# S5 chunk states: rows of 32 neighbouring groups for each chunk, in place of rows of chunks for each group

## The chip, the core and the metric

The kernel runs on one core of a Trainium2 chip. The metric is the device time in microseconds (us) of one execution of the whole program, in fp32; the median of three runs of the kernel before is 1691.3 us (1687.9 to 1693.93). The engines named below are PE (TensorE; PEld is its loading of the stationary operand, which runs beside PE), DVE (VectorE), ACT (ScalarE), POOL (GpSimd) and SP (SyncE, which here only issues DMAs).

## What is computed

One inference step of a trunk of four layers (S5, RetNet, Hyena, S5) on 128 context tokens and 256 latent tokens, 384 columns in all, with a model width of 1024. The change touches the two S5 layers (layer 0 and layer 3) alone. There the 1024 channels form 64 groups of 16, and each group drives a complex diagonal state of 64 numbers in two directions:

```python
bu_re = jnp.einsum('blgh,gph->blgp', u, bb_re)      # and bu_im
_, _, h_re, h_im = lax.associative_scan(combine, (a_re, a_im, bu_re, bu_im), axis=1)
y = (jnp.einsum('blgp,ghp->blgh', h_re, c_re) - jnp.einsum('blgp,ghp->blgh', h_im, c_im))
```

The second direction does the same on the reversed sequence, and the result is y of both plus d times u.

## The kernel before

**Chunks.** An S5 layer cuts the 384 tokens into 48 chunks of 8 (`NCH = 48`; the first `CC = 16` are context). Within a chunk the sum is a Toeplitz matmul; between chunks a state of 128 numbers (64 complex ones) for each group and direction is carried. These chunk states are the tile X. There are two halves of it (`Xs[0]` and `Xs[1]`, 32 groups each, `XH = 32`), and each is 128 partitions by 64 rows (2 directions times 32 groups) by `XP = 49` columns (chunk boundaries). So one group's states over all chunks lie side by side, and the states of neighbouring groups at one chunk are 49 numbers (196 bytes) apart.

**Who touches X, in order.**
- `use_p(b)` (one for every 8 groups) makes each chunk's own contribution: matmuls of U with PB (line 746), copies to Ss (line 748, ACT), transposes (line 755, PE), and a copy from PSUM into X (line 758, ACT: 384 numbers for each partition, 32 copies in both layers).
- `recur(q)` (line 769, once for each half q) carries the states from chunk to chunk on DVE. One round is line 792 (a shuffle that swaps real and imaginary parts, X to sw), 793 (X times A1 to m1), 794 (add m1 to the next X), 795 (sw times A2) and 796 (add sw to the next X), each on 64 numbers for each partition: 32 groups in two directions. There are 47 rounds in a call (31 for the latent chunks, 16 for the context), 188 in both layers. Context and latent rounds do not depend on each other and alternate until the context is done. A context's last round writes XF, a small tile of 64 neighbouring numbers, instead of X, and line 797 sends it out on the ACT queue.
- Lines 880 to 882 make y: for every group a matmul with U (880), one with X of the first direction (881) and one with X of the second (882). X is the stationary operand there: 48 columns, the states of one group at 48 chunks.

**What sets the order.** The program is written as plans (`PLAN0`, `PLAN1`): P is `use_p`, R is `recur`, U the input projection. R0 (half 0) stands after P3, R1 (half 1) after P7. The half's last copy (line 758) releases `recur`. After the plan come the gate matmuls (line 138, with line 161's cast on ACT, line 133's remainder on POOL, line 530 on ACT and line 531 on DVE for each of 8 blocks), which don't need X, and then lines 880 to 882. A scheduler with a timing model of its own places the instructions of each engine's queue; every queue then runs in its order. In layer 0 the DVE also makes CP (lines 628 and 629, `gen_c`), whose sums are added by DMAs issued on POOL (line 631) and whose inputs xc are loaded on the SP queue (line 686), between weight loads (line 152) and loads of Tt (line 850).

Of the kernel before, what the change touches and what calls it, by code (L numbers as in the profile page):

```python
# [10 lines left out]
F32 = mybir.dt.float32  # L11
# [15 lines left out]
NCH = T // Q  # L27
XP = NCH + 1
CC = NCTX // Q
# [7 lines left out]
NH = 2  # L37
# [67 lines left out]
def hybrid_trunk(ctx: ExitStack, tc: tile.TileContext, I, O, dbg=None, layers=(0, 1, 2, 3)):  # L105
    nc = tc.nc
    V, S, G, TE = nc.vector, nc.scalar, nc.gpsimd, nc.tensor
# [13 lines left out]
    def psm():  # L121
        return pm.tile([128, 512], F32, tag="m", name="psm")
# [9 lines left out]
    def gstt(out, a, b, op):  # L132
        G.tensor_tensor(out, a, b, op=op)  # L133
# [218 lines left out]
    def tick(n=1):  # L352
        for _ in range(n):
            if bg:
                bg.popleft()()
# [328 lines left out]
    def gen_c(j, hb, tb, rot, CP, xb, eng=V, add=G):  # L684
        xc = rot.tile([128, 2, 2, 4, 16], F32, tag="xc", name="xc")
        nc.sync.dma_start(xc, I["s5bc"][j, hb // 4, :, hb % 4, 1])
        expand_c(CP, rot, tb, xc, hb, xb, eng, add)
# [10 lines left out]
    def s5(i, j, nxt, begun=lambda: None):  # L698
        def mk(st, name, bufs=1, **kw):
            return st.enter_context(tc.tile_pool(name=f"{name}_{i}", bufs=bufs, reuse_waits="tile", **kw))  # L700
        ep = ExitStack()
        eU = ExitStack()
        pool = mk(eU, "s5", side="right") if j == 0 else mk(ep, "s5")
        U = pool.tile([128, 8, 8 * NCH + 16], F32, name="U")
        XH = 64 // NH
        Xs = [pool.tile([128, 2 * XH, XP], F32, name=f"X{q}") for q in range(NH)]
        XFs = [pool.tile([128, 2, XH], F32, name=f"XF{q}") for q in range(NH)]
        hpool = mk(ep, "s5h")
        h0 = load(pool, "h0", I["s5h0"][j], eng=nc.scalar)
# [29 lines left out]
        def use_p(b):  # L739
            Ss = ru.tile([128, 2, 512], F32, tag="Ss", name="Ss", bufs=1)  # L740
            for r in range(2):
                PB = PBs.pop(2 * b + r)
                ps = psm()
                for g in range(4):
                    o = 64 * (g % 2)
                    mark[0] = TE.matmul(ps[o:o + 64, (g // 2) * 256:(g // 2) * 256 + 256], U[:, b, (r * 4 + g) * NCH:(r * 4 + g) * NCH + 64],  # L746
                              PB[:, g].rearrange("p a b -> p (a b)"), start=True, stop=True)
                S.copy(Ss[:, r], ps)
            for hf in range(2):
                ps = psm()  # L750
                o = 64 * hf
                for g in range(4):
                    for d in range(2):
                        c = (g % 2) * 256 + d * 128
                        TE.transpose(ps[:, (d * 4 + g) * 64:(d * 4 + g) * 64 + 48],  # L755
                                     Ss[o:o + 48, g // 2, c:c + 128], ident[o:o + 48, o:o + 48])
                xb = Xs[b * 8 // XH][:, b * 8 % XH + hf, 1:2]
                S.copy(bass.AP(tensor=xb.tensor, offset=xb.offset,
                               ap=[xb.ap[0], [XH * XP - 1, 2], [2 * XP, 4], [1, NCH]]),
                       ps.rearrange("p (d g c) -> p d g c", d=2, g=4)[:, :, :, :48])  # L760

        def u_epi(m, ps):
# [7 lines left out]
        def recur(q):  # L770
            gs = slice(q * XH, (q + 1) * XH)
            A1, A2 = Av[:, 0, :, gs], Av[:, 1, :, gs]
            X, XF = Xs[q], XFs[q]
            Xb = X[:, 0, 0:1]
            V.tensor_copy(XF[:, 0], X[:, 0:XH, CC])
            V.tensor_copy(XF[:, 1], X[:, XH:2 * XH, 0])

            def view(c_f, c_b):
                return bass.AP(tensor=Xb.tensor, offset=Xb.offset + c_f,
                               ap=[Xb.ap[0], [XH * XP + c_b - c_f, 2], [XP, XH]])  # L780
            V.memset(view(0, CC), 0.0)
            V.tensor_copy(view(CC, NCH), h0.rearrange("p (d g) -> p d g", d=2)[:, :, gs])
            for k in range(NCH - CC - 1):
                for c0, n in ((CC, NCH - CC), (0, CC)):
                    if k >= n:
                        continue
                    c1 = c0 + n - 1
                    cur = view(c0 + k, c1 - k + 1)
                    dst = XF if k == n - 1 else view(c0 + k + 1, c1 - k)
                    sw = tmp.tile([128, 2, XH], F32, tag=f"sw{c0}{q}", name="sw")  # L790
                    m1 = tmp.tile([128, 2, XH], F32, tag=f"m1{c0}{q}", name="m1")
                    V.stream_shuffle(sw, cur, [(x + 16) % 32 for x in range(32)])  # L792
                    V.tensor_mul(m1, cur, A1)  # L793
                    V.tensor_add(dst, dst, m1)  # L794
                    V.tensor_mul(sw, sw, A2)  # L795
                    V.tensor_add(dst, dst, sw)  # L796
            nc.scalar.dma_start(O["ns5"][j].rearrange("p (d g) -> p d g", d=2)[:, :, gs], XF)
# [47 lines left out]
        def toeplitz(m):  # L845
            kdm = I["kd"][j * 8 + m]
            Tt = rot.tile([128, 8, 128], F32, tag="Tt", name="Tt")
            for t in range(8):
                src = bass.AP(tensor=kdm.tensor, offset=kdm.offset + (7 - t) * 16, ap=[[1920, 16], [240, 8], [1, 128]])
                nc.sync.dma_start(Tt[16 * t:16 * t + 16], src)  # L850
            Tm = rot.tile([128, 8, 128], F32, tag="Tm", name="Tm", bufs=TMB)
            for r in range(2):
                ps = psm()
                for g in range(4):
                    TE.transpose(ps[:, g * 128:(g + 1) * 128], Tt[:, r * 4 + g, :], ident)  # L855
                S.copy(Tm[:, r * 4:r * 4 + 4, :], ps.rearrange("p (g c) -> p g c", c=128))
            Tms.append(Tm)
        for m in range(TMB):
            toeplitz(m)
        for m in range(8):  # L860
            CP = []
            for r in range(2):
                c = rot.tile([128, 2, 4, 8, 16], F32, tag="CP", name="CP", bufs=CPB if j == 0 else CP1)
                if j == 0 and 2 * m + r not in SPL:
                    gen_c(j, 2 * m + r, tb, rot, c, 2, V, None)
                else:
                    (CQ if j else nc.sync).dma_start(c.rearrange("p d g e c -> p (d g e c)"), I["cpd"][2 * m + r])
                CP.append(c)
            Tm = Tms[m]
            hf = m % 2  # L870
            if hf == 0:
                pys = [psm(), psm()]
                Ys = rot.tile([128, 8, 8, 16], F32, tag="Ys", name="Ys", bufs=1)
            for r in range(2):
                for g in range(4):
                    gl = r * 4 + g
                    gg = m * 8 + gl
                    o = pys[r][64 * hf:64 * hf + 64, g * 128:(g + 1) * 128]
                    o48 = pys[r][64 * hf:64 * hf + 48, g * 128:(g + 1) * 128]
                    TE.matmul(o, U[:, m, gl * NCH:gl * NCH + 64], Tm[:, gl, :], start=True, stop=False)  # L880
                    TE.matmul(o48, Xs[gg // XH][:, gg % XH, 0:48], CP[r][:, 0, g].rearrange("p a b -> p (a b)"), start=False, stop=False)  # L881
                    TE.matmul(o48, Xs[gg // XH][:, XH + gg % XH, 1:49], CP[r][:, 1, g].rearrange("p a b -> p (a b)"), start=False, stop=True)  # L882
            if m + TMB < 8:
                toeplitz(m + TMB)
            tick(CT)
            if hf == 0:
                continue
            for r in range(2):
                S.copy(Ys[:, :, r * 4:r * 4 + 4, :], pys[r].rearrange("p (g t i) -> p t g i", g=4, t=8))
            for hf in range(2):  # L890
                fb = m - 1 + hf
                o = 64 * hf
                pg = psm()
                for t in range(8):
                    TE.transpose(pg[:, t * 64:t * 64 + 48], Ys[o:o + 48, t].rearrange("p a b -> p (a b)"),  # L895
                                 ident[o:o + 48, o:o + 48])
                y = pg.rearrange("p (t c) -> p c t", t=8)[:, :48, :]
                x2 = t384("gx2").rearrange("p (c t) -> p c t", t=8)
                gf = t384("gf")
                gv = gf.rearrange("p (c t) -> p c t", t=8)  # L900
                S.activation(x2, y, AF.Square, scale=math.sqrt(0.044715))
                V.scalar_tensor_tensor(x2, x2, 1.0, y, op0=OP.add, op1=OP.mult)
                S.activation(x2, x2, AF.Tanh, scale=math.sqrt(2.0 / math.pi))
                V.scalar_tensor_tensor(gv, x2, 1.0, y, op0=OP.add, op1=OP.mult)
                put(g_parts, fb, gf)
                gstt(sgate[:, fb, :], gf, sgate[:, fb, :], OP.mult)
# [670 lines left out]
```

## Time and profile before

| what | us |
|---|---|
| median of three runs | 1691.3 |
| the profiled execution | 1695.14 |
| its span, first to last instruction | 1693.3 |
| PE busy in it | 1488.7 (88%) |
| DVE busy in it | 1288.4 (76%) |
| ACT busy, POOL busy | 688.8 (41%), 660.6 (39%) |

The span is divided by layer: layer 0 runs to about 420 us, layer 3 from about 1400 us to the end. A share of the whole span says little here, since the two stages with the recurrence (about 167 to 326 us and 1466 to 1572 us) have other limits than the dense matmuls that fill the rest. They are read by windows, by the instructions' durations line by line, and by what PE waited for.

### The profile page before, as it was taken

The page shows a single profiled execution, that of the slowest core. Times are in us where ns is not written, and L with a number is a line of the kernel's source. Part 1 is how long each engine was busy: PE and PEld are TensorE (multiplying, and loading weights), DVE is VectorE, ACT ScalarE, POOL GpSimd, SP SyncE. Part 2 cuts the span into 40 slices and gives each one's busy share as a digit, 9 for nine tenths or more (in the row PEclk, how much of TensorE's full clock was granted, in tenths as well). Part 3 has the DMA queues.
Part 4 walks back from the last instruction along what each step waited for, and adds up shares of the span by engine and source line. Part 5 has one row for each costly group of instructions (what it writes and reads, how often), then busy time and mean ns, then how long its engine had stood idle before and what let it go on. Part 6 is the DMA issues. An engine that isn't in the chain of part 4 may idle for free. (4 is left out here: it accounts for less than half of the span.)

```text
span 1693.3 us, 27807 instructions
## 1 busy us (share of the span) xinstructions
PE 1488.7 (88%) x10370; PEld 1320.6 (78%) x10370; DVE 1288.4 (76%) x3123; ACT 688.8 (41%) x1275; POOL 660.6 (39%) x484
## 2 busy tenths in 40 slices
PE   5778776799689998999979999999999998976996
PEld 3555564677579888889969989989899797675996
DVE  8957998569787777755878988888798855399355
ACT  2534321333333333335455545454555444421343
POOL 2111231213375756651325655655576131230221
PEclk7888887899899999999989999999999999987998
DMA  8578469844555555544333222222322463755431
GB/s 346 172 227 242 132 167 256 206 144 174 187 173 200 189 198 189 179 152 135 130 114 111 87 75 83 97 94 78 100 88 80 145 240 110 239 145 179 125 125 63
DMA packets 107807, 261.41 MB, mean 154 GB/s; under 512 B 28535, under 2 KB 68568, under 8 KB 88088
## 3 DMA queue, kind: packets, MB, share of 16 engines
q1 hardware_dynamic: 80768, 200.12, 36.1%
q0 software_dynamic: 11984, 34.87, 7.5%
q10 hardware_dynamic: 14920, 24.65, 4.0%
q8 instruction: 82, 1.34, 0.3%
q14 instruction: 53, 0.43, 0.1%
HBM read 220.37 MB, written 30.83 MB: 148 GB/s over the span
## 5 line engine op out<-in xcount | busy, mean ns | idle before, releaser
L133 POOL TENSOR_TENSOR wl<-wr,wh 128x1024 fp32r<-128x1024 f32 (+2 forms) x99 | 248.3, 2513 | 322.2 <-ACT wh L161 294.4
L161 ACT CAST wh<-wr 128x1024 fp32r<-128x1024 f32 (+4 forms) x211 | 215.7, 1029 | 292.7 <-PE psd L138 215.2
L138 PE MATMUL psd<-hh,wh 128*128 128x384 f32 x880 | 305.9, 349 | 17.6 <-ACT wh L161 7.5
L138 PE MATMUL psd<-hh,wl 128*128 128x384 f32 x880 | 304.5, 347 | 11.2 <-POOL wl L133 8.8
L138 PE MATMUL psd<-hl,wh 128*128 128x384 f32 x880 | 304.6, 346 | 6.5 <-DVE hl L469 6.4
L148 DVE TENSOR_TENSOR wl<-wr,wh 128x1024 fp32r<-128x1024 f32 (+3 forms) x112 | 146.4, 1309 | 73.3 <-ACT wh L161 72.8
L138 PEld LDWEIGHTS psd<-hh,wh 128*128 128x128 f32 x880 | 169.1, 193 | 29.6 <-issue 12.9
L138 PEld LDWEIGHTS psd<-hh,wl 128*128 128x128 f32 x880 | 169.1, 192 | 20.1 <-POOL wl L133 10.5
L138 PEld LDWEIGHTS psd<-hl,wh 128*128 128x128 f32 x880 | 169.1, 192 | 15.8 <-DVE hl L469 9.2
L138 PE MATMUL psd<-wl,hh 128*128 128x256 f32 x384 | 110.3, 289 | 5.2 <-DVE wl L148 3.8
L138 PE MATMUL psd<-wh,hh 128*128 128x256 f32 x384 | 110.9, 293 | 4.1 <-DVE g L531 2.8
L138 PE MATMUL psd<-wh,hl 128*128 128x256 f32 x384 | 109.0, 286 | 0.0
L378 PE MATMUL psn<-wr,sgc 128*32 128x256 f32 x640 | 58.3, 450 | 45.4 <-DMA wr<-in_mod_w_dram 37.9
L138 PE MATMUL psd<-zb,wh 128*128 128x384 f32 x240 | 80.9, 338 | 0.0
L138 PEld LDWEIGHTS psd<-wl,hh 128*128 128x128 f32 x384 | 74.1, 193 | 6.9 <-DVE wl L148 4.7
L138 PEld LDWEIGHTS psd<-wh,hh 128*128 128x128 f32 x384 | 73.6, 193 | 6.2 <-DVE g L531 3.5
L138 PEld LDWEIGHTS psd<-wh,hl 128*128 128x128 f32 x384 | 74.1, 193 | 0.1
L629 DVE TENSOR_TENSOR xt<-BI,xc 128x512 f32<-128x512 f32 x52 | 45.2, 870 | 37.0 <-POOL CP L633 16.6
L378 PEld LDWEIGHTS psn<-wr,sgc 128*32 128x32 f32 x640 | 20.0, 121 | 67.3 <-DMA wr<-in_mod_w_dram 41.2
L633 POOL TENSOR_TENSOR BP<-BP,xt 128x512 f32<-128x512 f32 x32 | 46.0, 1437 | 63.7 <-DVE xt L629 37.7
L629 DVE TENSOR_TENSOR xt<-FI,bc 128x512 f32<-128x512 f32 x64 | 48.8, 768 | 26.7 <-DMA CP<-xt 9.0
L631 POOL DMA_DIRECT2D CP<-xt x32 | 27.6, 905 | 101.0 <-DVE X L796 28.7
(388 smaller groups left out, 4069.6 us busy)
## 6 DMA issues: line engine op xcount, KB each, us to landing
wr<-in_mod_w_dram SPq DMA_DIRECT2D x40, 1024.0 KB
wr<-in_hy_w_in_dram SPq DMA_DIRECT2D x32, 1024.0 KB
wr<-in_ret_w_in_dram SPq DMA_DIRECT2D x24, 1024.0 KB
wr<-in_s_w_in_dram SPq DMA_DIRECT2D x16, 1024.0 KB
wm<-in_mod_w_dram SPq DMA_DIRECT2D x8, 1024.0 KB
CP<-xt POOLq DMA_DIRECT2D x32, 256.0 KB, 7.2
Tt<-scratch_kd_dram SPq DMA_DIRECT2D x128, 64.0 KB
wr<-in_s_w_glu_dram SPq DMA_DIRECT2D x8, 1024.0 KB
```

The source lines that it names most:

```text
L133: G.tensor_tensor(out, a, b, op=op)
L138: TE.matmul(out, lhs[a], rhs[b], start=start and i == 0, stop=stop and i == len(combos) - 1)
L148: V.tensor_sub(out, a, b)
L161: S.copy(hi, ap)
L378: TE.matmul(ps[q * 32:(q + 1) * 32, :256], sg[:, kb, 6 - 2 * u:38 - 2 * u], raw[:, kb, :], start=u == 0 and k2 == 0, stop=u == 3 and k2 == 1)
L629: eng.tensor_tensor(t, c2, x[:, 1].unsqueeze(2).to_broadcast([128, 4, 8, 16]), op=OP.mult)
L631: nc.gpsimd.dma_start(out, t, accum_op=OP.add)
L633: add.tensor_tensor(out, out, t, op=OP.add)
```

## The change

X gets the index order direction, chunk, group: 128 partitions by 2 by 49 by 32. The 32 groups of one chunk and direction are now 32 neighbouring numbers, and one group's consecutive chunks are 32 numbers (128 bytes) apart. The size is the same. All that reads or writes X follows: the ACT copy of line 758 writes runs of 48 with a step of 32 where it wrote neighbouring numbers; all DVE operands of `recur` on X are two runs of 32 neighbours where they were 64 single numbers 49 apart; the stationary operand of lines 881 and 882 is 48 numbers with a step of 32 where it was 48 neighbours. No instruction is added or removed.

```diff
-        Xs = [pool.tile([128, 2 * XH, XP], F32, name=f"X{q}") for q in range(NH)]
+        Xs = [pool.tile([128, 2, XP, XH], F32, name=f"X{q}") for q in range(NH)]
...
-                xb = Xs[b * 8 // XH][:, b * 8 % XH + hf, 1:2]
+                xb = Xs[b * 8 // XH][:, 0, 1:2, b * 8 % XH + hf]
                 S.copy(bass.AP(tensor=xb.tensor, offset=xb.offset,
-                               ap=[xb.ap[0], [XH * XP - 1, 2], [2 * XP, 4], [1, NCH]]),
+                               ap=[xb.ap[0], [(XP - 1) * XH, 2], [2, 4], [XH, NCH]]),
                        ps.rearrange("p (d g c) -> p d g c", d=2, g=4)[:, :, :, :48])
...
-            Xb = X[:, 0, 0:1]
-            V.tensor_copy(XF[:, 0], X[:, 0:XH, CC])
-            V.tensor_copy(XF[:, 1], X[:, XH:2 * XH, 0])
+            Xb = X[:, 0, 0, 0:1]
+            V.tensor_copy(XF[:, 0], X[:, 0, CC])
+            V.tensor_copy(XF[:, 1], X[:, 1, 0])
 
             def view(c_f, c_b):
-                return bass.AP(tensor=Xb.tensor, offset=Xb.offset + c_f,
-                               ap=[Xb.ap[0], [XH * XP + c_b - c_f, 2], [XP, XH]])
+                return bass.AP(tensor=Xb.tensor, offset=Xb.offset + c_f * XH,
+                               ap=[Xb.ap[0], [(XP + c_b - c_f) * XH, 2], [1, XH]])
...
-                    TE.matmul(o48, Xs[gg // XH][:, gg % XH, 0:48], CP[r][:, 0, g].rearrange("p a b -> p (a b)"), start=False, stop=False)
-                    TE.matmul(o48, Xs[gg // XH][:, XH + gg % XH, 1:49], CP[r][:, 1, g].rearrange("p a b -> p (a b)"), start=False, stop=True)
+                    TE.matmul(o48, Xs[gg // XH][:, 0, 0:48, gg % XH], CP[r][:, 0, g].rearrange("p a b -> p (a b)"), start=False, stop=False)
+                    TE.matmul(o48, Xs[gg // XH][:, 1, 1:49, gg % XH], CP[r][:, 1, g].rearrange("p a b -> p (a b)"), start=False, stop=True)
```

The scheduler orders some instructions anew. Two places matter for the prediction. The first is DVE in layer 3, where R1 (half 1, X1_14481) begins among the rounds of R0 (half 0, X0_14480). The kernel before, from a round of R0 to the first rounds of both:

```order
L794 TENSOR_TENSOR X0_14480<-X0_14480,m1_15057 128x2x32
L796 TENSOR_TENSOR X0_14480<-X0_14480,sw_15063 128x2x32
L775 COPY XF1_14483<-X1_14481 128x32
L776 COPY XF1_14483<-X1_14481 128x32
L781 MEMSET X1_14481 128x2x32
L796 TENSOR_TENSOR X0_14480<-X0_14480,sw_15056 128x2x32
L792 STREAM_SHUFFLE sw_15077<-X0_14480 128x64
```

The same place in the changed kernel:

```order
L795 TENSOR_TENSOR sw_15070<-sw_15070,A1_4514 128x64
L794 TENSOR_TENSOR X0_14480<-X0_14480,m1_15071 128x2x32
L775 COPY XF1_14483<-X1_14481 128x32
L776 COPY XF1_14483<-X1_14481 128x32
L781 MEMSET X1_14481 128x2x32
L796 TENSOR_TENSOR X0_14480<-X0_14480,sw_15077 128x2x32
L796 TENSOR_TENSOR X0_14480<-X0_14480,sw_15070 128x2x32
```

R1's first copy stands behind 22 rounds of R0 before and behind 24 now. From there to R0's last round 60 rounds of either half follow before (25 of R0, 35 of R1) and 57 now (23 and 34); 12 rounds of R1 come last before, 13 now. In layer 0, 79 rounds stand from R0's first to its last, before and now.

The second place is the ACT queue of layer 3 at the gate blocks, where the issue of line 797 (which waits for half 0's context states, XF0) moves behind one more block (lines 161 and 530):

```order
 L530 ACTIVATE silu_15849<-psd_15820 128x384
+L161 CAST wh_15921<-wr_15918 128x1024
+L530 ACTIVATE silu_15883<-psd_15854 128x384
+L856 COPY Tm_16111<-psm_16112 128x512
 L797 DMA out_ns5_dram<-XF0_14482 256x1x32
-L530 ACTIVATE silu_15883<-psd_15854 128x384
-L161 CAST wh_15921<-wr_15918 128x1024
+L856 COPY Tm_16111<-psm_16118 128x512
 L161 CAST wh_15953<-wr_15918 128x1024
```

The third block's cast and activation stood behind line 797's wait and now stand ahead of it.

## Rows read from the trace of the kernel before

**Rows 1.** Windows: stretch, its length, busy PE, PEld, DVE, ACT, POOL, clock, DMA share, GB/s.

```profile
240.00:275.00 35.00, 16.77 (x104) 12.98 (x104) 33.84 (x154) 1.36 (x3) 10.62 (x9) 0.67 0.79 203
270.00:280.00 10.00, 3.56 (x24) 2.17 (x25) 9.89 (x60) 0.00 (x0) 1.70 (x2) 0.50 1.02 290
1520.00:1548.00 28.00, 20.03 (x146) 15.09 (x144) 28.00 (x164) 3.59 (x6) 4.23 (x2) 0.89 0.70 204
1548.00:1572.00 24.00, 18.05 (x150) 17.41 (x151) 21.20 (x124) 7.12 (x14) 3.06 (x5) 0.77 0.56 156
```

**Rows 2.** Instructions by line, DVE: count, minimum/median/maximum ns, first and last start.

```profile
L793 DVE TENSOR_TENSOR m<-X,A x188: 239/255/2344, 169.0 to 1570.3; 128x64 f32<-128x64 f32 x188
L794 DVE TENSOR_TENSOR X<-X,m x184: 250/266/5432, 174.4 to 1571.1; 128x64 f32<-128x64 f32 x184
L794 DVE TENSOR_TENSOR XF<-XF,m x4: 218/228/233, 211.4 to 1546.6; 128x64 f32<-128x64 f32 x4
L781 DVE MEMSET X<- x4: 112/112/112, 167.4 to 1487.6; 128x64 f32 x4
L338 DVE MEMSET ones<- x1: 165/165/165, 0.8 to 0.8; 128x128 f32 x1
```

**Rows 3.** Timeline of DVE, one round of R1 alone: start us, us, what.

```profile
1559.82 0.26 DVE L792 STREAM_SHUFFLE sw<-X 128x64 f32<-128x64 f32 x1
1560.00 0.26 DVE L793 TENSOR_TENSOR m<-X,A 128x64 f32<-128x64 f32 x1
1560.17 0.22 DVE L795 TENSOR_TENSOR sw<-sw,A 128x64 f32<-128x64 f32 x1
1560.30 0.27 DVE L794 TENSOR_TENSOR X<-X,m 128x64 f32<-128x64 f32 x1
...
1560.92 0.26 DVE L792 STREAM_SHUFFLE sw<-X 128x64 f32<-128x64 f32 x1
```

**Rows 4.** Layer 3: shuffles until R1 begins; timeline, with idle time before and its releaser.

```profile
L792 DVE STREAM_SHUFFLE sw<-X x22: 248/254/272, 1466.8 to 1486.1; 128x64 f32<-128x64 f32 x22
...
1485.27 1.00 ACT L758 COPY X<-psm 128x384 f32<-128x384 f32 x2 [3.40 <-PE psm L755]
1487.31 0.17 DVE L775 COPY XF<-X 128x32 f32<-128x32 f32 x1
1509.68 0.49 ACT L530 ACTIVATE silu<-psd 128x384 f32<-128x384 f32 x1 [17.52 <-DVE X L796]
1554.97 0.66 PE L881 MATMUL psm<-CP,X 128*48 128x128 f32 x2 [4.78 <-DVE X L796]
1571.70 0.57 DVE L796 TENSOR_TENSOR X<-X,sw 128x64 f32<-128x64 f32 x1
1574.94 0.38 PE L881 MATMUL psm<-CP,X 128*48 128x128 f32 x2
```

**Rows 5.** Layer 0: timeline of PE at the first use of X; waits of SP's queue.

```profile
275.34 1.94 PE L378 MATMUL psn<-wr,sgc 128*32 128x256 f32 x16 [8.03 <-DMA wr<-in_mod_w_dram]
278.37 0.66 PE L881 MATMUL psm<-CP,X 128*48 128x128 f32 x2 [1.10 <-DVE X L796]
...
SPq L686 <- DVE X L794: 10.9, 1, 10.9
```

**Rows 6.** Stationary loads and ACT copies by line (as rows 2); two steps of PE's timeline.

```profile
L881 PEld LDWEIGHTS psm<-CP,X x256: 119/123/203, 278.4 to 1609.9; 128*48 128x48 f32 x128
L1253 PEld LDWEIGHTS psm<-ident,ac x96: 138/196/217, 889.5 to 1345.1; 128*128 128x128 f32 x96
L764 ACT COPY us<-psd x14: 469/479/491, 75.9 to 1467.4; 128x384 f32<-128x384 f32 x14
L764 ACT COPY us<-xb x2: 925/931/937, 1433.8 to 1434.7; 128x384 f32<-128x384 f32 x2
...
296.57 0.38 PE L882 MATMUL psm<-CP,X 128*48 128x128 f32 x2
296.79 0.38 PE L880 MATMUL psm<-Tm,U 128*64 128x128 f32 x2
```

## The prediction, made before the changed kernel ran

> **What bounds the kernel now.** I read the windows of the two stages with the recurrence first, then the durations of the recurrence's instructions, then what PE waited for when it first needed X. In [rows 1] DVE is busy for 33.84 of 35 us in layer 0 and for all 28 us of a stretch of layer 3, while PE, which bounds most of the kernel, is busy for 16.77 and 20.03 us. So here, and only here, DVE sets the pace. The reader should then see where that ends. In layer 3 PE's first matmul with X starts at 1554.97 after 4.78 us of waiting for line 796, the last add of the recurrence [rows 4]: all that follows hangs on R0's end. R1's end, at 1571.70 + 0.57 = 1572.3, is needed by the matmul at 1574.94, so it has 2.7 us to spare. In layer 0 the same first matmul waited only 1.10 us for DVE, right behind 8.03 us for a weight load [rows 5], with the DMA engines fully busy there (share 1.02, [rows 1]); DVE is one of two late things.
>
> **What the change takes off DVE.** Every round reads or writes X four times (lines 792, 793, 794, 796). The trace has the same instructions on neighbouring numbers. Line 794 takes 266 ns on X and 228 ns where it works on XF [rows 2]; line 793, which only reads X, takes 255, and line 795, on two neighbouring operands, 0.22 us [rows 3]. Instructions on DVE overlap, so what counts is the step from one start to the next. In [rows 3] the steps are 0.18 after the shuffle, 0.17 after line 793, and 0.13 after line 795, the one without X. So X costs 0.045 us a step, four times a round: 0.18 us of a round that takes 1.10 us alone (1559.82 to 1560.92). No row has a shuffle on neighbours in SBUF; its gain lies between 0 and 0.045, and I take 0.045, since it reads X exactly as line 793 does. With 0 a round would gain 0.135. For 188 rounds that is 25 to 34 us of DVE; the rest is where these rounds stand.
>
> **Layer 3.** R0's 22 rounds up to R1's start run from 1466.8 to 1487.31, some 0.85 us each apart from one 2 us stall [rows 4]. With 24 rounds of 0.67 us and that stall DVE reaches R1 at about 1485, but R1 needs the last copies of line 758, which PE's own work releases and which end at 1486.27 [rows 4]. So R1 starts 1.0 us earlier and the rest of that gain is lost in a wait. From there to R0's end before were 1554.97 - 1487.31 = 67.7 us with 60 rounds; now there are 57. Three rounds fewer are 2.5 us (0.84 each), and 57 x 0.18 = 10.3. Together 1.0 + 2.5 + 10.3 = 13.8 us, with 0.135 a round 11.2. For PE to take it, its gate blocks must be ready 9 us earlier than now (13.8 less the 4.78 us that it waited). They wait for DVE's line 531, which comes earlier with the rounds, and for ACT, which stood 17.52 us behind line 797 [rows 4]; the new order puts a block ahead of that wait. Should PE not gain anything of its own, only the 4.8 us are left. I take 13. What is late next: R1's end. After R0's end 13 rounds of R1 remain where 12 did; before they took 17.3 us, now 17.3 + 1 x 0.92 - 12 x 0.18 = 16.1, and PE needs its 20 us for half 0 as before, so R1 stays hidden.
>
> **Layer 0.** 79 rounds up to R0's end are 79 x 0.18 = 14.2 us at most. The least is 1.1 us, if the weight load ahead of the first matmul with X doesn't move [rows 5]. But that load was itself late because of DVE: it is issued on SP, which stood 10.9 us behind an xc load (line 686) that waited for DVE [rows 5]. DVE had done 58 rounds by then (some 10 us). So the queue starts 10 us earlier, and then runs into DMA engines that had been idle for part of that wait and are full afterwards. I take 9 of 1.1 to 14.2. Line 631's sums and the POOL remainders behind them come earlier with DVE and need no term.
>
> **What it adds.** *ACT's copies* (line 758) write single numbers 128 bytes apart. Reading SBUF with a step of 32 bytes doubles a copy, 931 against 479 ns [rows 6], so the bound is 0.45 us, of which two copies ahead of each R stand on the path: up to 1.8 us in layer 3. But writes look free: a memset of 64 single numbers of X takes 112 ns and one of 128 neighbours 165 [rows 2], 0.83 ns for each further number and nothing for the step. I take 0. *PE's loads of X* now read 48 single numbers. A load of 48 neighbours takes 123 ns and hides behind matmuls that start every 109 ns (two in 296.57 to 296.79, [rows 6]). Line 1253 loads 128 neighbours in 138 ns or 128 numbers with a step of two in 196, 0.45 ns more for each; DVE's surcharge is 0.6 ns for each number (39 ns for 64), ACT's 1.18 ns (452 for 384). With 0.45 to 1.18 ns a load of X takes 145 to 180 ns, below the 196 of line 1253, which still run at some 115 ns a matmul. So I take 0, with up to 10 ns a load, or 512 x 10 = 5 us, as the bound.
>
> [...]
>
> **The sum.** 13 + 9 = 22 us off the profiled execution's 1695.14 is 1673; that execution lies 3.8 us above the median, and from the median it is 1691.3 - 22 = 1669.3. I predict 1669.5.
>
> **Rivals.** *DMA keeps layer 0:* the full DMA engines eat nearly all of the 9 us, and 13.5 to 15 us remain, 1677. For it: share 1.02 and the 8.03 us wait. Against: the SP wait of 10.9 us on DVE. *PE keeps layer 3:* its gate blocks and weight loads stay late, and 9 + 5 = 14 remain, 1677 too. *PE's loads become the bound:* a step of 128 bytes is one that no row shows, and could be far dearer than 1.18 ns a number. A load of 196 ns holds matmuls at about 115, so a recorded load less some 80 ns is what it occupies. The gain of 22 us is spread over 512 loads (256 a layer, each layer bound by PE from its first use of X on), 43 ns each: it is gone when a load occupies 152 ns, so records 232, at 2.3 ns a number, twice ACT's surcharge. At three times it (3.5 ns, 293 ns recorded, 213 occupied) 104 x 512 = 53 us are lost and 31 remain: 1722. Against it are three surcharges from three engines, all lower. *The step isn't what slows DVE:* then nothing changes, 1691. The XF rows speak against it.
>
> **How the numbers follow.** The forecast has 0.65, DMA in layer 0 0.12, PE in layer 3 0.07, PE's loads beyond the break-even 0.08, loads with a few us of price 0.03, no effect 0.05. The range goes from both DVE gains in full (13.8 + 14.2 = 28, and some 2 us of PE at a fuller clock) to the least in both (4.8 + 1.1 = 6): 1661 to 1686. It leaves out 0.08, 0.05 and some of the rest. About 0.3% (5 us) is what a measurement tells from no change: faster 0.85 (all but the last cases), same 0.06, slower 0.09.
>
> **What would show it.** Right: lines 793, 794 and 796 at about 216 to 228 ns and the shuffle near 220; line 758 still at 485; loads of X below 190 with matmuls still every 109 ns; the first matmul with X in layer 3 some 13 us earlier against the layer's start, and DVE waiting shortly for line 758 before R1. Wrong: loads of X above 230 ns and a step above 109 after 1555; DVE idle in layer 3's gate blocks behind line 531; in layer 0 a wait of PE for a weight load where DVE's had been.

## The result, and the profile after

The changed kernel took 1672.47 us (median of four runs, 1671.17 to 1675.14) against 1692.62 for the kernel before (1687.9 to 1695.8): a ratio of 0.9887 with a 95% interval of 0.9863 to 0.9911, or 15 to 23 us less. Run again beside three variants it gave 0.9874 (0.9849 to 0.99). Forecast were 1669.5 in a range of 1661 to 1686.

Durations in the profile after, by line (count, minimum/median/maximum ns, first and last start), the counterpart of [rows 2] and of the loads in [rows 6]:

```profile
L792 DVE STREAM_SHUFFLE sw<-X x188: 208/217/226, 166.8 to 1551.4; 128x64 f32<-128x64 f32 x188
L793 DVE TENSOR_TENSOR m<-X,A x188: 201/208/2441, 166.9 to 1551.6; 128x64 f32<-128x64 f32 x188
L794 DVE TENSOR_TENSOR X<-X,m x184: 204/211/2384, 172.3 to 1552.3; 128x64 f32<-128x64 f32 x184
L796 DVE TENSOR_TENSOR X<-X,sw x184: 163/210/2104, 173.3 to 1552.6; 128x64 f32<-128x64 f32 x184
L758 ACT COPY X<-psm x32: 818/864/938, 112.2 to 1471.6; 128x384 f32<-128x384 f32 x32
L881 PEld LDWEIGHTS psm<-CP,X x256: 157/162/205, 263.2 to 1586.8; 128*48 128x48 f32 x128
```

The lines of the kernel before that [rows 2] and [rows 6] don't show:

```profile
L792 DVE STREAM_SHUFFLE sw<-X x188: 248/264/298, 168.8 to 1570.1; 128x64 f32<-128x64 f32 x188
L796 DVE TENSOR_TENSOR X<-X,sw x184: 248/266/2414, 175.4 to 1571.7; 128x64 f32<-128x64 f32 x184
L758 ACT COPY X<-psm x32: 482/485/510, 113.6 to 1485.8; 128x384 f32<-128x384 f32 x32
```

Everything that DVE does to X is at least as fast as its work on neighbouring operands was before; both new prices are there too. ACT's copy went from 485 to 864 ns, PE's load from 123 to 162.

One round that DVE works on alone, from the timeline (start us, us, what), the counterpart of [rows 3]:

```profile
261.55 0.22 DVE L792 STREAM_SHUFFLE sw<-X 128x64 f32<-128x64 f32 x1
261.68 0.21 DVE L793 TENSOR_TENSOR m<-X,A 128x64 f32<-128x64 f32 x1
261.81 0.22 DVE L795 TENSOR_TENSOR sw<-sw,A 128x64 f32<-128x64 f32 x1
261.95 0.22 DVE L794 TENSOR_TENSOR X<-X,m 128x64 f32<-128x64 f32 x1
262.20 0.23 DVE L796 TENSOR_TENSOR X<-X,sw 128x64 f32<-128x64 f32 x1
...
262.47 0.22 DVE L792 STREAM_SHUFFLE sw<-X 128x64 f32<-128x64 f32 x1
```

The first three steps are now 0.13 to 0.14 us each (the last two, 0.25 and 0.27, each follow an instruction whose result they need), and the round takes 0.92 us: the 0.18 us that the prediction counted, the shuffle's share in it.

PE around the first matmul with X, from the timeline, first layer 0, then layer 3, the counterparts of [rows 5] and [rows 4]; then windows of layer 3 (stretch, length, busy PE, PEld, DVE, ACT, POOL, granted clock, DMA share, GB/s):

```profile
250.46 1.93 PE L378 MATMUL psn<-wr,sgc 128*32 128x256 f32 x16 [1.02 <-DVE sw L795]
261.31 1.93 PE L378 MATMUL psn<-wr,sgc 128*32 128x256 f32 x16 [8.93 <-DMA wr<-in_mod_w_dram]
263.18 0.66 PE L881 MATMUL psm<-CP,X 128*48 128x128 f32 x2
...
1522.14 1.93 PE L378 MATMUL psn<-wr,sgc 128*32 128x256 f32 x16 [5.74 <-DMA wr<-in_mod_w_dram]
1528.69 0.67 PE L881 MATMUL psm<-CP,X 128*48 128x128 f32 x2 [4.62 <-DVE X L796]
...
1514.00:1524.00 10.00, 4.26 (x53) 1.83 (x51) 10.00 (x84) 0.49 (x1) 0.00 (x0) 0.86 0.71 175
1524.00:1529.00 5.00, 0.38 (x6) 0.30 (x3) 4.96 (x45) 1.72 (x3) 0.00 (x0) 0.50 0.95 377
1529.00:1534.00 5.00, 5.00 (x24) 4.54 (x22) 4.43 (x24) 0.00 (x0) 0.00 (x0) 0.50 0.06 19
1534.00:1539.00 5.00, 5.00 (x31) 4.79 (x32) 4.20 (x31) 0.51 (x2) 0.58 (x1) 0.58 0.34 105
1539.00:1544.00 5.00, 5.00 (x47) 4.86 (x46) 0.00 (x0) 1.36 (x4) 1.05 (x2) 1.00 0.53 170
```

In layer 0 PE no longer waits for DVE: the first matmul with X follows a weight block whose load was waited for 8.93 us. The whole place stands 15.2 us earlier (278.37 to 263.18). In layer 3 PE still waits for R0, 4.62 us, and the place stands 26.3 us earlier. Behind it PE runs at a granted clock of 0.50 until about 1538. The clock was down already when that wait began: shorter windows show 1.00 over 1520 to 1521, 0.56 over 1521 to 1522 and 0.50 over 1522 to 1524, so it fell at about 1521, late in the 5.74 us for which PE stood idle ahead of the weight block. It fell before too (0.50 over 1550 to 1555), but half as many steps behind the first matmul with X ran slow (table below), and half 0 of the layer, from the first matmul with X to the first with the X of half 1, takes 33.4 us where it took 30.2: 3.2 us of the gain are given back. Some 0.5 of that is not the clock's: four matmuls of line 385, 0.54 us in the changed kernel run again (a_ctl below), stood ahead of the first matmul with X before and stand in half 0 now.

Starts of a few instructions tell where the gain is. The last two columns count from R0's first copy (line 775) in layer 3; "half-clock steps" are steps of 0.21 us between matmuls of lines 880 to 882 right behind the first one with X in layer 3 (at full clock a step is 0.109).

| kernel | layer 0: layout | first 881 | layer 3: R0 starts | half-clock steps | first 881 after R0 | last 882 after R0 |
|---|---|---|---|---|---|---|
| before | old | 278.4 | 1466.3 | 19 | 88.7 | 143.9 |
| changed | new | 263.2 | 1453.1 | 38 | 75.6 | 134.1 |
| changed, again (a_ctl) | new | 269.4 | 1454.0 | 17 | 74.7 | 130.5 |
| e_l0 | new | 268.6 | 1453.6 | 22 | 88.7 | 144.4 |
| e_l3 | old | 271.6 | 1460.0 | 16 | 74.7 | 130.4 |
| e_step8 | new, 8 bytes | 269.2 | 1458.4 | 24 | 75.1 | 132.1 |
| e_no795 | new | 246.9 | 1455.4 | 0 | 64.4 | 121.3 |
| e_copya | new | 265.7 | 1452.5 | 19 | 78.2 | 134.2 |
| e_pad | new | 267.5 | 1457.5 | 18 | 74.9 | 131.1 |
| e_warm | new | 263.3 | 1451.0 | 0 | 78.3 | 132.3 |
| e_late15 | new | 262.0 | 1451.5 | 21 | 71.7 | 129.1 |
| e_late17 | new | 269.0 | 1449.0 | 24 | 69.5 | 131.4 |
| e_cw | new | 266.2 | 1455.6 | 0 | 78.9 | 132.9 |
| e_best | new | 266.7 | 1457.6 | 0 | 76.5 | 131.6 |

### The profile page after: what moved, and what is told of

Read it like the earlier page. It is cut to its first block, busy times and chain, and to the rows that moved or that the text cites. A ratio compares the mean times of both kernels' runs of the same rounds, so it can differ in the third digit from the quotient of the medians.

```text
span 1670.0 us, 27794 instructions
## 1 busy us (share of the span) xinstructions
PE 1480.2 (89%) x10370; PEld 1316.1 (79%) x10370; DVE 1254.5 (75%) x3123; ACT 695.5 (42%) x1275; POOL 662.3 (40%) x484
## 5 line engine op out<-in xcount | busy, mean ns | idle before, releaser
L628 DVE TENSOR_TENSOR CP<-B,xc 128x512 f32<-128x512 f32 x52 | 54.3, 1076 | 18.8 <-DMA scratch_cpd_dram<-CP 9.7
```

The source lines that it names most:

```text
L628: eng.tensor_tensor(out, c1, x[:, 0].unsqueeze(2).to_broadcast([128, 4, 8, 16]), op=OP.mult)
```

## The experiments

My theory was the prediction's: the step through X is what slowed DVE, both layers gain on their own, PE's dearer loads are hidden. The rivals that were left: the gain is the new order's and not the layout's, layer 0's gain is lost to DMA, and the time given back in layer 3 belongs to the change.

No run has the old layout in the new order, so the first rival is met by counting. In layer 3, between R0's first copy and the first matmul with X, DVE finishes 83 rounds before and 82 in the changed kernel, with line 531 eight times in both. The steps of the rounds' instructions there, each from one start to the next start on DVE, sum to 83.9 us before and 71.0 after; one round fewer is worth about 1 us of that, and the rest lies in the same instructions taking less time. That the order played no other part, on ACT and PE, is not shown.

**One layer at a time.** Two runs chose the layout by layer (`j == 0` in e_l0, `j == 1` in e_l3; "..." stands for lines left out, here and below):

```diff
-        XH = 64 // NH
+        XH = 64 // NH; NEW = j == 0; ...
-        Xs = [pool.tile([128, 2, XP, XH], F32, name=f"X{q}") for q in range(NH)]
+        Xs = [pool.tile([128, 2, XP, XH] if NEW else [128, 2, XH, XP], F32, name=f"X{q}") for q in range(NH)]
...
```

> New layout in layer 0 only, old layout in layer 3. In the trace of the changed kernel the matmuls run 14.0 us earlier than before from 450 us on until layer 3 begins. If the two layers add up, the same 14 us must be left at the end here, and layer 3 takes as long as before: 14 us less than the kernel before, ratio 0.9917. Rival: the layer 0 gain depends on nothing but is partly given back in layer 3 (its weights come no earlier): 0 to 8 us less, ratio 0.995 to 1.

> New layout in layer 3 only, old layout in layer 0. If the layers add up: 9.3 us less than the kernel before (23.1 in the traces less the 13.8 that were there when layer 3 began), ratio 0.9945, with the first matmul of line 881 in layer 3 about 13 us earlier against R0's first copy than before, and half the clock for some 9 us behind it, so that 3 to 4 us are given back. Rival: the 9 us at half clock are chance and not tied to this layer's new order; then 12 to 13 us are left, ratio 0.9925.

New in layer 0 alone: 1682.04 us against 1693.54, ratio 0.9926 (0.9901 to 0.9951). New in layer 3 alone: 1681.93, ratio 0.9922 (0.9891 to 0.9952). Each layer gains on its own, 12.5 and 13.2 us by the ratios with some 4 to 5 either way; together they are no less than the whole change, so neither layer's gain hangs on the other. One execution of e_l0 has both layouts side by side, the shuffle in layer 0 (new) and in layer 3 (old), by line as above:

```profile
L792 DVE STREAM_SHUFFLE sw<-X x94: 210/218/228, 169.8 to 308.7; 128x64 f32<-128x64 f32 x94
L792 DVE STREAM_SHUFFLE sw<-X x94: 252/263/313, 1454.1 to 1557.9; 128x64 f32<-128x64 f32 x94
```

The second expectation decided the question of the half clock, by its profile (the interval of its time holds both answers): layer 3 of e_l3 has the same instructions in the same order as in the changed kernel, and there the half clock lasted 16 steps and layer 3 130.4 us, not 38 and 134.1. The rival was right: the 38 steps don't belong to the layout or the order. The changed kernel run again showed 17 steps and 130.5 us. What sets the length from one execution to the next is not shown.

> The changed kernel itself, as the ruler for the three that run beside it, and for whether the gain and the stretch at half clock repeat. Ratio to the kernel before between 0.985 and 0.991; layer 3 from R0's first copy to line 882's last matmul between 130 and 134.1 us, by how long the half clock lasts behind the first matmul with X (16 to 38 steps of 0.213 us in the profiles so far).

It took 1671.31 us against 1693.18, as expected. Its timeline of PE, where the pace changes at 1532.5 already and not at 1538:

```profile
1528.70 0.66 PE L881 MATMUL psm<-CP,X 128*48 128x128 f32 x2 [4.55 <-DVE X L796]
...
1531.29 0.63 PE L881 MATMUL psm<-CP,X 128*48 128x128 f32 x2
1532.51 0.38 PE L881 MATMUL psm<-CP,X 128*48 128x128 f32 x2
```

e_l3 showed a second thing. Its layer 0 is the kernel before, instruction for instruction, and yet layer 3 began at 1460.0 instead of 1466.3. So one and the same layer 0 varies by several us from run to run: its first matmul with X came at 271.6 here and at 278.4 before.

**How far apart is too far.** The two directions interleaved, so that DVE steps 8 bytes, ACT and PE 256:

```diff
-        Xs = [pool.tile([128, 2, XP, XH], F32, name=f"X{q}") for q in range(NH)]
+        Xs = [pool.tile([128, XP, XH, 2], F32, name=f"X{q}") for q in range(NH)]
...
```

> Both directions of X interleaved: DVE steps 8 bytes through X, ACT and PE 256 bytes (64 numbers) instead of 128. Theory A, a number pays for itself as soon as its neighbour isn't next to it: lines 793, 794, 796 and the shuffle back at 250 to 266 ns, the time near the kernel before (1685 to 1695). [...] For PE: if a step's price doesn't grow with its length, line 881's loads stay at 157 to 165 ns and ACT's copies of line 758 at 864; if it does, loads go above 200 and the last 256 matmuls with X start further apart than 109 ns. [...]

1677.41 us, ratio 0.9902 (0.9869 to 0.9934). By line:

```profile
L792 DVE STREAM_SHUFFLE sw<-X x188: 209/218/230, 171.6 to 1551.1; 128x64 f32<-128x64 f32 x188
L758 ACT COPY X<-psm x32: 813/866/914, 116.1 to 1475.8; 128x384 f32<-128x384 f32 x32
L881 PEld LDWEIGHTS psm<-CP,X x256: 157/160/203, 269.2 to 1590.2; 128*48 128x48 f32 x128
L1253 PEld LDWEIGHTS psm<-ident,ac x96: 137/196/217, 881.2 to 1336.7; 128*128 128x128 f32 x96
```

Theory A is out for DVE: at 8 bytes the shuffle takes 218 ns, against 217 for neighbours and 264 at the 196 bytes of the old rows; lines 793, 794 and 796 take 208 to 213. The time lies below the 1685 to 1695 of theory A and above the 1672.47 of the changed kernel; the order of the instructions is another one here, and what the difference comes from is not shown. ACT's copy and PE's load are much the same at 256 bytes as at 128 (866 against 864 ns, 160 against 162), so their price doesn't grow from the one step to the other. PE's load pays at 8 bytes already: two thirds of line 1253's loads step 8 bytes, and in the changed kernel's trace they take 195 to 217 ns, the loads of neighbours 137 to 162.

**Is 128 bytes a bad step?** Rows of 33 numbers in layer 3, 32 in layer 0:

```diff
-        Xs = [pool.tile([128, 2, XP, XH], F32, name=f"X{q}") for q in range(NH)]
+        Xs = [pool.tile([128, 2, XP, XH + j], F32, name=f"X{q}") for q in range(NH)]
...
```

> Changed kernel with rows of 33 numbers for X in layer 3 (132 bytes) and 32 (128 bytes) in layer 0; the order of the instructions is the same. [...] Theory B, 128 bytes is a bad step because all numbers fall on the same part of the memory: loads near 123 to 140 ns and copies well under 864 in layer 3, unchanged in layer 0.

One run, 1673.44 us. Layer 0 and layer 3 of it, by line:

```profile
L881 PEld LDWEIGHTS psm<-CP,X x128: 157/161/199, 267.5 to 342.8; 128*48 128x48 f32 x128
L881 PEld LDWEIGHTS psm<-CP,X x128: 162/163/199, 1532.4 to 1588.2; 128*48 128x48 f32 x128
L758 ACT COPY X<-psm x16: 810/868/955, 116.0 to 202.6; 128x384 f32<-128x384 f32 x16
L758 ACT COPY X<-psm x16: 857/894/967, 1438.4 to 1475.3; 128x384 f32<-128x384 f32 x16
```

Theory B is out: 132 bytes are no better than 128 (163 against 161 ns for the loads, 894 against 868 for the copies).

**ACT's copies.** They walk the groups first, so that they write every second number; no instruction moves:

```diff
-                               ap=[xb.ap[0], [(XP - 1) * XH, 2], [2, 4], [XH, NCH]]),
-                       ps.rearrange("p (d g c) -> p d g c", d=2, g=4)[:, :, :, :48])
+                               ap=[xb.ap[0], [(XP - 1) * XH, 2], [XH, NCH], [2, 4]]),
+                       ps.rearrange("p (d g c) -> p d c g", d=2, g=4)[:, :, :48])
```

> Changed kernel with ACT's copies of line 758 walking groups first: they write every second number (8 bytes) and read PSUM 256 bytes apart; no instruction changes its place. [...] Theory B, a write pays per number that isn't beside the one before it, or reading PSUM with a step costs as much: 820 ns or more. Either way the two copies ahead of each half's first round are worth 0.4 to 0.8 us a half, so the time stays within 1.5 us of the changed kernel (1671 to 1673), since three of the four starts don't set an end.

```profile
L758 ACT COPY X<-psm x32: 482/494/509, 113.3 to 1473.8; 128x384 f32<-128x384 f32 x32
```

Theory B is out: 494 ns with PSUM read 256 bytes apart, against 485 in the kernel before. The time was 1668.89 against 1696.4, ratio 0.9834 (0.9798 to 0.9869), better than I expected. I don't call that shown: the changed kernel did not run beside it, layer 3 took 134.2 us in its profile (DVE waited 3.2 us there for the copies ahead of R1, against 0.9 in the changed kernel), and e_cw below, with the same copies, gave no gain over the changed kernel beside it.

**The clock behind the wait.** 36 extra matmuls in the wait of layer 3, each on a chunk of X that R0's last rounds write:

```diff
...
+ [TE.matmul(o[:8], Xs[0][:, 0, c - 7:c + 1, 0], CP[0][:, 0, 0].rearrange("p a b -> p (a b)"), start=True, stop=True) for c in range(41, 47) for _ in range(6) if j and gg == 0]; ...
```

> Changed kernel with 36 small extra matmuls in layer 3 in the wait ahead of the first matmul with X; each needs a chunk of X that the last rounds of R0 write, so PE works on and off there, and their results are overwritten. Theory A, the 3.2 us that the changed kernel gives back behind this place come from PE's lower clock after its idle time: the clock stays at full, half 0 takes 30.2 us or less (33.4 in the changed kernel), and layer 3 from R0's first copy to line 882's last matmul takes 131 us or less (134.4). Theory B, the lower clock is not tied to the idle time: 38 or so steps at half clock remain and the 134.4 us too. By A the time is 1 to 3 us below the changed kernel.

Windows, then PE's timeline:

```profile
1515.00:1520.00 5.00, 5.00 (x43) 2.91 (x47) 5.00 (x44) 0.00 (x0) 0.00 (x0) 0.66 0.18 28
1520.00:1525.00 5.00, 5.00 (x52) 3.54 (x44) 5.00 (x45) 0.00 (x0) 0.00 (x0) 1.00 0.94 383
1525.00:1530.00 5.00, 5.00 (x55) 4.00 (x53) 4.28 (x24) 1.62 (x3) 0.00 (x0) 1.00 0.47 114
...
1526.30 2.78 PE L880 MATMUL psm<-CP,X 128*8 128x128 f32 x24
1529.28 0.38 PE L881 MATMUL psm<-CP,X 128*48 128x128 f32 x2
```

The clock did not stay at full: PE had idled 4.4 us before the extra matmuls began at 1514.95, and 1515 to 1520 shows 0.66. But with PE busy from there on it was back at 1.00 from 1520 to the first matmul with X, no half-clock step followed, and half 0 took 28.9 us (1.8 to 4.5 less than in the two runs of the changed kernel). So the slow steps belong to the idle time ahead of line 881: all four runs without them in the table had these matmuls there or (e_no795) no wait, and all ten others had the wait and 16 steps or more. But the first matmul came 78.3 us after R0's start, some 3 later than in the changed kernel: R0's last add was done at 1525.6, but the extra matmuls ran on until 1529.0, ahead of line 881. 1671.64 us, ratio 0.986 (0.9831 to 0.9888): nothing is left of it that can be measured.

**What bounds it now.** Line 795 left out:

```diff
-                    V.tensor_mul(sw, sw, A2)
+                    pass
```

> Changed kernel without line 795: the product of the shuffled state with A2 is left out, so the imaginary parts of the recurrence's factor are missing; 188 DVE instructions of 0.13 us a step fewer (25 us of DVE). If DVE still set both layers' ends all of it would come off: about 22 us less than the changed kernel, 1650. What I expect: in layer 0 the first matmul with X already stood right behind a weight load (8.9 us wait), and in layer 3 a weight load ended 4.6 us ahead of it, so only 5 to 10 us come off (1662 to 1668), with the wait before line 881 gone in layer 3 and a wait for weights in its place.

1660.6 us, ratio 0.9799 (0.976 to 0.9839): 12 us less than the changed kernel's median, and 15 by the ratios to the kernel before, since the two did not run side by side. That is about half of the 25 us that DVE saved and a little more than I expected. Its timeline of PE in layer 0, then in layer 3:

```profile
246.94 0.67 PE L881 MATMUL psm<-CP,X 128*48 128x128 f32 x2 [1.98 <-DVE X L796]
...
1501.05 0.66 PE L138 MATMUL psd<-hh,wh 128*128 128x384 f32 x1 [8.41 <-DVE X L794]
...
1518.78 1.07 PE L378 MATMUL psn<-wr,sgc 128*32 128x256 f32 x16
1519.78 0.46 PE L881 MATMUL psm<-CP,X 128*48 128x128 f32 x2
```

In layer 3 PE's own blocks now run up to the first matmul with X, and the wait for weights that I expected in its place did not come. That doesn't free the layer from DVE: a gate block 19 us earlier waited 8.41 us for it, and layer 3 took 121.3 us, 9 to 13 less than in the two runs of the changed kernel. In layer 0 the first matmul with X came 16 us earlier than in the changed kernel, because DVE was done earlier and the order puts it ahead of the weight blocks; yet layer 3 began no earlier than elsewhere (1455.4). So a faster recurrence in layer 0 was not kept in this order.

**R1 held back.** In the changed kernel R1 ends 9.3 us before PE needs it (1552.78 against 1562.08) while PE waits for R0. Two runs hold R1's rounds in layer 3 (`rmark[17]` in e_late17, the longer hold; `rmark[15]` in e_late15):

```diff
...
-                recur(n)
+                with tc.issue_after(rmark[17].ins) if j and n else ExitStack(): recur(n)
```

> Changed kernel with R1's rounds in layer 3 held until R0 has done 34 of its 47 rounds (24 before): 26 rounds of R1 stand ahead of R0's end instead of 34. In the changed kernel R1 ends 9.3 us before PE needs it while PE waits 4.6 us for R0. Eight rounds at 0.67 us less, and some 10 rounds of R0 alone at 0.92 instead of 0.67 make R0's end 3 us earlier; PE takes that, since its last weight block is done 4.6 us ahead. Theory A: the first matmul with X 3 us earlier against R0's first copy (75.6 us in the changed kernel), and R1 still hidden: 2 to 6 us less than the changed kernel, clock included. Theory B, the rounds of R0 alone cost as much as the interleaved ones give, or R1 comes late: no gain or a loss of up to 3 us, with a wait of PE for R1 ahead of its half.

> R1 held until R0 has done 32 rounds, without the other two edits. If PE's lower clock is what ate the gain of the longer hold (half 0 took 36.0 us there): first matmul with X at 72 to 74 us after R0's first copy, half 0 in 30 to 34 us, layer 3 in 130 to 132. If R1's end binds: PE waits for it ahead of its half, layer 3 in 131 or more.

With the longer hold the first matmul with X came at 69.5 us, 6 earlier. Then R1's end met PE's need, in DVE's timeline and PE's:

```profile
1553.90 0.57 DVE L796 TENSOR_TENSOR X<-X,sw 128x64 f32<-128x64 f32 x1
...
1553.84 0.62 PE L138 MATMUL psd<-gh,wh 128*128 128x384 f32 x2 [2.22 <-ACT gh L174]
1554.52 0.67 PE L881 MATMUL psm<-CP,X 128*48 128x128 f32 x2
```

PE took half 1 the moment R1's last add was done, in steps of 0.21 us again (two in 1554.98 to 1555.41), and layer 3 took 131.4 us. Just ahead of it PE had stood 2.22 us for ACT, so R1 is not all that held it. The shorter hold gave 71.7 and 129.1 us, a little better than expected. The times are 1673.42 (ratio 0.9869, 0.9825 to 0.9913) and 1670.2 (0.9865, 0.984 to 0.9891): a gain of 1.4 us in a layer doesn't rise above what layer 0 varies.

**All together**, with copies and extra matmuls, without and with the shorter hold:

> Changed kernel with ACT's copies walking groups first and with the extra matmuls in layer 3. If both small gains are real: copies at 494 ns, half 0 of layer 3 in 28.9 us with 7 or fewer steps at half clock, and 2 to 4 us less than the changed kernel beside it (ratio to it 0.9976 to 0.9988). Rival: ACT's copies set no end, and the extra matmuls delay PE's weight blocks as much as the clock gives: within 1 us of it.

> The same with R1 held in layer 3 until R0 has done 32 of its rounds: 30 rounds of R1 ahead of R0's end (34 in the changed kernel, 26 in the run that held it longer, where R1's end, 104.9 us after R0's first copy, met the first use of its half at 105.6). Expected: first matmul with X 72 to 74 us after R0's first copy, R1's end 101 to 103, the half at 102 to 104, layer 3 in 127 to 130 us: 4 to 6 us less than the changed kernel beside it. Rival: R1's end binds here too, and PE waits for it; then no more than the kernel with copies and extra matmuls alone.

e_cw took 1673.76 us (0.9881, 0.9854 to 0.9908), e_best 1666.11 (0.9844, 0.9813 to 0.9875), the changed kernel beside them 1671.31 (0.9874, 0.9849 to 0.99). e_cw's median lies 2.4 us above the changed kernel's, with intervals that overlap: the gain isn't there, and the rival comes nearest. e_best has the lowest median, but its interval overlaps with the changed kernel's, and the profile of it, its slowest run, shows layer 3 in 131.6 us and the first matmul with X at 76.5, later than I expected (DVE stood idle for 3.5 us there ahead of line 531, waiting for ACT's line 530). A version that beats the changed kernel is not shown.

## Why the prediction was right, point by point

**The round.** Right to the hundredth for a round alone: 1.10 to 0.92 us, the shuffle gaining as much as line 793. The steps of 0.13 and 0.17 on neighbouring rows of one timeline were the price; the durations (47 ns less for the shuffle and for line 793, 55 and 56 for the adds) say the same. But most rounds of layer 3 stand in pairs, one of each half, and there the price was too high: a pair went from 1.67 us (1549.99 to 1551.66 before) to 1.35 (1526.00 to 1527.35 after), 0.16 a round and not 0.18.

**Layer 3, predicted 13.** The first matmul with X came 13.1 us earlier against R0's start (88.7 to 75.6), and 14.0 in the profiles of e_l3 and a_ctl. Two parts of the 13.8 were off and made up for each other: from R1's start to R0's end 11.6 us came off and not 12.8 (67.7 to 56.1, by the price above), and R1 began 1.5 to 2.4 us earlier instead of 1.0, in the first profile after the short wait for line 758 that was named as a sign (0.9 us). What was kept at the layer's end is 9.8 us in the first profile and 13.5 in the other two. The prediction had a term for PE's own lateness (13.8 less 4.78 must be found ahead), and that held: the last weight block was done 4.6 us early. It had none for the clock, which was down at the first matmul with X in the kernel before too; how long it stays down differs between executions, and the first profile drew the long one.

**R1's end, given 2.7 us to spare.** It stayed hidden, as predicted, but by a misreading. The matmul at 1574.94 [rows 4] is the 49th of 128 of line 881 in that layer and still works on half 0; the first with the X of half 1 is the 65th:

```profile
1585.15 0.38 PE L881 MATMUL psm<-CP,X 128*48 128x128 f32 x2
```

So R1 had 12.9 us to spare before, and half 0 takes PE 30.2 us, not 20. The 16.1 us for R1's last rounds were too few as well: they took 24.1 and, in a_ctl, 21.4, because line 902 stands between them on DVE and waited for ACT (7.3 us in the first profile). With the 20 us that the prediction gave PE, R1 would have come late; with the true 33.4 and 30.7 it had 9.3 us to spare in both.

**Layer 0, predicted 9 of 1.1 to 14.2.** The two first profiles give 15.2 at the first matmul with X, above my bound, and 13.2 at the start of layer 3. That pair flatters: in the two profiles with the old layer 0 layer 3 began at 1466.3 and 1460.0, a mean of 1463.1; in the ten with the new one (without the 8-byte step and line 795's run) at 1449.0 to 1457.6, a mean of 1453.5. That is 9.6 us (8.8 at the first matmul with X), with only two runs on one side, and e_l0's 12.5 with its interval agrees. The 9 was picked between 1.1 and 14.2, so that it fits this well is in part luck. The mechanism fits the one named: SP's wait of 10.9 us for DVE ahead of line 686 [rows 5] is gone, its longest there now 4.1 and that for a DMA. The 10.9 flatters too: with the same old layer 0 the longest such wait in e_l3 was 6.5 us. That the weight load came earlier because of this wait is argued, not shown by a run of its own. Waits of SP's queue in the same stretch after, two rows, then in e_l3 (us in total, times, longest):

```profile
SPq L686 <- DMA wr<-in_mod_w_dram: 4.1, 1, 4.1
SPq L686 <- DVE m L793: 3.8, 2, 3.3
...
SPq L686 <- DVE sw L792: 6.5, 1, 6.5
```

One sign of mine misled: I wrote that a wait of PE for a weight load in DVE's place would speak against it. It came (8.93 us), and the gain with it, since the load itself had moved.

**ACT's copies, taken as 0 with a bound of 0.45 us.** This term failed. I drew "writes look free" from a memset of 64 numbers that takes 112 ns with a step [rows 2]. It takes 112 without one as well, but a copy's writes cost 0.38 us here, nearly the bound. It didn't decide anything: two copies ahead of each half are 0.8 us, and with the copies back at 494 ns no gain can be told.

**PE's loads, 145 to 180 ns and hidden.** 162 ns, and hidden to the hundredth where it can be told: from the first matmul with the X of half 1 to the last of line 882 in layer 3, at full clock throughout, it is 25.07 us before and after and 25.06 in a_ctl. The third rival needed 232.

**The sum and the rivals.** 22 us were predicted; the medians differ by 20.2 us, and in the run again by 21.9. PE still waits for a DMA ahead of the first matmul with X in layer 0, but the gain that this was to eat is there. PE did not keep layer 3. No effect and PE's loads are out. The chance of 0.85 for faster had the right case under it.

## What to carry to other kernels

When two engines read one tile along different axes, lay it out for the one that sets the pace, and look at whether the other hides its price behind its own work: here 47 to 56 ns came off each of the four DVE instructions on X in a round, 188 rounds in all, and 39 ns more on each stationary load of X vanished under matmuls (25.07 us for them in half 1 of layer 3, before and after). Read an access's price from the step between two starts, not from a busy sum, and price each engine's reads and writes by rows of that engine. Before a gain of a few us is credited to a mechanism from one pair of profiles, look how far an unchanged stretch differs between two of them.

## What the runs showed of the hardware that I had not expected

- DVE and ACT pay next to nothing at 8 bytes (218 against 217 ns; 494 against 485). DVE pays at 196 bytes (264), and ACT's price is much the same at 128, 132 and 256 bytes (864, 894 and 866). ACT pays for writes with a step too: 0.99 ns for each number (379 ns for 384), close to the 1.18 that the prediction worked out for its reads from [rows 6]. PE pays at 8 bytes already (196 against 137 ns for 128 numbers) and 0.8 ns a number at 128 to 256 bytes (39 ns for 48).
- Behind much the same idle time and with the same instructions PE worked in steps of 0.21 us, where 0.109 is a step at full clock, for 16 to 38 steps. With extra matmuls in that time the clock fell as well (0.66 over 1515 to 1520 in e_warm), but was back at 1.00 from 1520 on, before the first matmul with X.
- With one and the same layer 0, layer 3 began at 1460.0 in one execution and 1466.3 in another, and in the ten with the new layer 0 at anything from 1449.0 to 1457.6. What differs between them was not settled.
